# Turning the gated activations by DMA, as planes of 16-bit halves, instead of on TensorE

## The chip, the cores and the metric

The kernel runs on one core of one Trainium2 chip. The metric is the device time of one execution in microseconds (us). The engines are named as the profile names them: PE is TensorE (PEld its weight loads), DVE is VectorE, ACT is ScalarE, POOL is GpSimd, SP is SyncE. PE, DVE and ACT do the arithmetic here; SP and POOL, and now ACT too, issue DMAs.

## The reference

One layer of a decoder: RMSNorm, three token mixers, merged by gates and projected, with a residual; then RMSNorm and a SwiGLU feed-forward layer with a residual. The change touches the feed-forward part only:

```python
D_MODEL = 2048; SEQ = 256; D_FF = 5632
h2 = rmsnorm(x, g_ffn)                       # 256 x 2048, float32
gu = h2 @ w_gu                               # 256 x 11264
x = x + (jax.nn.silu(gu[..., :D_FF]) * gu[..., D_FF:]) @ w_down
```

The gated activations `a = silu(g) * u` are 256 x 5632 in float32. The product with `w_gu` leaves the 256 tokens on partitions; the product with `w_down` needs `a` with the feed-forward index on partitions. So every block of `a` has to be transposed.

## The kernel before

The kernel is written in Python over a tile framework. The framework allocates the tiles, puts in the semaphores, and orders each engine's instructions by a planner that works with estimated durations; `keep_in_program_order` pins an instruction to its place. Each engine then runs its own instructions strictly in order.

Each float32 product is done as three reduced-precision matmuls (`product`, lines 164 to 169): high part times high part (L167), high times low (L168), low times high (L169). So every block of weights is split before use (`split`, L104 and L105): ACT casts it into `w_hi`, DVE subtracts to get `w_lo`. A block of weights is 128 x 2 x 512 float32, and there are five buffers each of `w_hi` and `w_lo`. ACT can split a block only when PE has read the buffer of five blocks before.

The stage that matters computes `g` and `u`. It is a loop over 11 chunks `c` of 512 feed-forward columns. `project_pair` computes one chunk for both halves of the tokens, with one level of a Strassen-like scheme on part of the blocks; it makes 22 weight blocks by calls of `parts`, eighteen for its own chunk and four (`begin_pair`) ahead for the next. In the order of the program the blocks are: f5 (two, from the tile `u`), two plain ones (`w_raw`), f6 (two, `u`), a plain one, f7 (two, `g_raw`), a plain one, f3 (two, `g_raw`), two plain ones, f4 (two, `u`), two plain ones, and the four of `begin_pair` (`g_raw`). A form block is read by six matmuls, a plain one by twelve: 180 matmuls in a chunk.

Small side jobs are generators in the list `stages`. Each call of `parts` runs the one at the front of the list to its next `yield` (`advance`). That is how `to_a(c, sg)`, appended after chunk `c`, is spread over the blocks of chunk `c+1`. `sg` are two tiles of 128 tokens x 512 columns, written by ACT (silu, L959) and DVE (L960).

Before the change `to_a` transposes with PE: `transpose4` (L185) does four 128 x 128 transposes of one `sg` tile into a PSUM tile `tr` (L189). For the chunks that are used first in the next stage (`ORDER[:EARLY]`, chunks 0, 1 and 2) `a.put` splits the result straight out of PSUM into `a_hi` and `a_lo`. For the other eight, ACT copies it into an SBUF tile (L950) and POOL issues its store to `a_mem` in device memory (L951), to be fetched and split in the next stage. `half_kb()` gives 128 x 512 float32 tiles out of twelve buffers.

During this stage SP issues the weight loads (L102), and POOL issues the stores of `a_mem` and two accumulating DMAs per chunk (L360).

Of the kernel before, what the change touches and what calls it, by code (L numbers as in the profile page):

```python
# [8 lines left out]

F32 = mybir.dt.float32  # L10
F32R = mybir.dt.float32r
AF = mybir.ActivationFunctionType
ALU = mybir.AluOpType
AX = mybir.AxisListType
# [3 lines left out]
P = 128  # L18
D = 2048
S = 256  # L20
NT = S // P
# [5 lines left out]
D_FF = 5632  # L27
NF = D_FF // P
NB = 512
# [25 lines left out]
def hybrid_block(ctx: ExitStack, tc: tile.TileContext, x, g_mix, w_in, q_gain, k_gain, w_branch, w_out,  # L55
                 g_ffn, w_gu, w_down, rel_bias, onehot, extra, out):
    nc = tc.nc
# [20 lines left out]
    def pool(stack, name, side, bufs=1):  # L78
        return stack.enter_context(tc.tile_pool(name=name, bufs=bufs, side=side, reuse_waits="tile"))

    h2_stack, ph1, pm, pgx = ExitStack(), ExitStack(), ExitStack(), ExitStack()
# [6 lines left out]
    def half_kb(dt=F32):  # L88

        return scratch.tile([P, NB], dt, name="sc")  # L90
# [13 lines left out]
    def split(hi, lo, src, pin=False):  # L104
        for op in nc.scalar.copy(hi, src), nc.vector.tensor_sub(lo, src, hi.bitcast(F32)):  # L105
            if pin:
                tc.keep_in_program_order(op)
# [5 lines left out]
    def raw_weights(w, row0, c, col0):  # L113
        raw = wpool.tile([P, 2, NB], F32, name="w_raw", bufs=4)
        return raw, nc.sync.dma_start(raw, block(w, row0 // P + c, col0))

    def weights(w, row0, k0, nk, col0, there=()):

        for i, c in enumerate(range(k0, nk, 2)):
            raw = there[i] if i < len(there) else raw_weights(w, row0, c, col0)[0]  # L120
            hi = wpool.tile([P, 2, NB], F32R, name="w_hi")
            lo = wpool.tile([P, 2, NB], F32R, name="w_lo")
            split(hi, lo, raw)
# [47 lines left out]
    def rsqrt_mean(dst, ss, n, cols):  # L171
# [3 lines left out]
        y = small.tile([P, cols], F32, name=f"rs_y{cols}")  # L175
        nc.scalar.activation(y, v, AF.Ln)
        nc.scalar.activation(y, y, AF.Exp, scale=-0.5)
        t = small.tile([P, cols], F32, name=f"rs_t{cols}")
# [6 lines left out]
    def transpose4(src):  # L185

        pt = tr.tile([P, 4, P], F32, name="tr")
        for i in range(4):
            nc.tensor.transpose(pt[:, i, :], src[:, i * P:(i + 1) * P], ident)  # L189
        return pt  # L190


    class Columns:


        def __init__(self, pl, name, nk):
            self.hi, self.lo = (pl.tile([P, nk, S], F32R, name=f"{name}_{n}") for n in ("hi", "lo"))

# [20 lines left out]
    class Sums:  # L219
# [8 lines left out]
        def place(self, pl, c):  # L228
            self.s[c] = [pl.tile([P, 4, S], F32R, name=f"{self.name}_s{n}{c}") for n in ("hi", "lo")]

# [14 lines left out]
    class Chunks(Sums):  # L245
# [9 lines left out]
        def place(self, pl, c):  # L255
            if c in self.wc:
                super().place(pl, c)
                self.t[c] = [[pl.tile(sh, F32R, name=f"{self.name}_{t}{n}{c}") for n in ("hi", "lo")]
                             for t, sh in enumerate(([P, 4, P], [P, 2, P]))]
            else:  # L260
                self.t[c] = [pl.tile([P, 4, S], F32R, name=f"{self.name}_{n}{c}") for n in ("hi", "lo")]

# [137 lines left out]
    h = Columns(p1, "h", KT)  # L400
# [13 lines left out]
    def to_h(acts, src, c, t, g, by_scalar=False):  # L414
# [3 lines left out]
        if by_scalar:  # L418
            for i in range(4):
                nc.scalar.activation(tmp[:, i], pt[:, i], AF.Copy, scale=g[:, 4 * c + i:4 * c + i + 1])  # L420
        else:
# [4 lines left out]
    def squares(xc, dst, c, pin=False):  # L426
        for t in range(NT):
            sq = nc.scalar.activation(half_kb(), xc[t], AF.Square, accum_out=dst[:, t, c:c + 1])
            if pin:
# [85 lines left out]
    with tc.manual_schedule(engines={mybir.EngineType.PE, mybir.EngineType.DVE, mybir.EngineType.Activation}):  # L515
# [16 lines left out]
        turned = [transpose4(xs[1][0])]  # L532
# [103 lines left out]
    def stick_breaking(hl, qT, kT, v):  # L636
# [7 lines left out]
        l = pa.tile([P, n], F32, name="p", bufs=1)  # L644
        nc.scalar.activation(l, z[:, :n], AF.Abs)
        nc.scalar.activation(l, l, AF.Exp, scale=-1.0)
        nc.scalar.activation(l, l, AF.Ln, bias=1.0)
# [267 lines left out]
    pm.close()  # L915
    pr = pool(ctx, "pr", "right")
    gd = pool(ctx, "gd", "right", 4)
    rstd2 = small.tile([P, NT], F32, name="rstd2", bufs=1)

    def second_norm():  # L920
# [11 lines left out]
    a_mem = dram.tile([NF // 4, P, 4, S], F32, name="a_mem")  # L932

    WD = (4, 6, 8)
    ORDER = [0, 1, 2, 4, 3, 6, 5, 8, 7, 9, 10]
    EARLY = 3
    a = Chunks(None, "a", NF // 4, WD, False)

    for c in ORDER[:EARLY]:
        a.place(pe, c)  # L940

    def to_a(c, srcs):
        for t in range(NT):
            pt = transpose4(srcs[t])
            if c in ORDER[:EARLY]:
                a.put(c, t, pt)
                yield
                continue
            st = half_kb().rearrange("p (k q) -> p k q", k=4)
            nc.scalar.copy(st, pt)  # L950
            nc.gpsimd.dma_start(a_mem[c, :, :, t * P:(t + 1) * P], st)  # L951
            yield

    for c in range(D_FF // NB):
        nxt = (h2, w_gu, (c + 1) * NB, D_FF + (c + 1) * NB) if c + 1 < D_FF // NB else None
        (g0, g1_, u0, u1), ahead = project_pair(h2, w_gu, c * NB, D_FF + c * NB, ahead, nxt)
        sg = [half_kb() for _ in range(NT)]
        for t, (g, u) in enumerate(((g0, u0), (g1_, u1))):
            nc.scalar.activation(sg[t], g, AF.Silu, scale=rstd2[:, t:t + 1])  # L959
            nc.vector.scalar_tensor_tensor(sg[t], u, rstd2[:, t:t + 1], sg[t], op0=ALU.mult, op1=ALU.mult)  # L960
        stages.append(to_a(c, sg))
# [179 lines left out]
```

## Time and profile before

| what | value |
|---|---|
| median of three runs | 1362.64 us (1362.42 to 1362.77) |
| the profiled execution | 1362.37 us |
| its span, first to last instruction | 1360.7 us |
| busy: PE, DVE, ACT | 1352.9, 1150.0, 878.8 us |
| granted TensorE clock | 1.0 throughout |
| mean DMA traffic | 241 GB/s |

Shares of busy time are means over the whole span. A line of the profile names engine, line of the kernel, operation, output and inputs, and the idle time of the engine ahead of it with what ended it. Busy times of PE include the pipelined ends of matmuls, so a sum of durations is more than the time that they take one behind another; the distance between two starts is what a matmul costs.

### The profile page before, as it was taken

The page shows a single profiled execution, that of the slowest core. Times are in us where ns is not written, and L with a number is a line of the kernel's source. Part 1 is how long each engine was busy: PE and PEld are TensorE (multiplying, and loading weights), DVE is VectorE, ACT ScalarE, POOL GpSimd, SP SyncE. Part 2 cuts the span into 40 slices and gives each one's busy share as a digit, 9 for nine tenths or more (in the row PEclk, how much of TensorE's full clock was granted, in tenths as well). Part 3 has the DMA queues.
Part 4 walks back from the last instruction along what each step waited for, and adds up shares of the span by engine and source line. Part 5 has one row for each costly group of instructions (what it writes and reads, how often), then busy time and mean ns, then how long its engine had stood idle before and what let it go on. Part 6 is the DMA issues. An engine that isn't in the chain of part 4 may idle for free.

```text
span 1360.7 us, 17886 instructions
## 1 busy us (share of the span) xinstructions
PE 1352.9 (99%) x6404; PEld 1181.1 (87%) x6404; DVE 1150.0 (85%) x1225; ACT 878.8 (65%) x1137; POOL 103.0 (8%) x164
## 2 busy tenths in 40 slices
PE   9999999999999999999999999999999999999998
PEld 7888888888888888888888888888888888888887
DVE  7888797866998887876789999999999998896885
ACT  7677877766876765445557666766666675664453
POOL 1100000000011112100100000010000010000000
PEclk9999999999999999999999999999999999999999
DMA  8775657566778788877797777778787876787653
GB/s 281 286 250 163 229 156 262 143 216 229 247 256 287 247 257 300 298 238 222 233 331 260 257 237 250 224 250 278 253 271 254 272 214 221 240 290 258 200 178 102
DMA packets 93016, 327.92 MB, mean 241 GB/s; under 512 B 11168, under 2 KB 12784, under 8 KB 92928
## 3 DMA queue, kind: packets, MB, share of 16 engines
q1 hardware_dynamic: 76896, 275.29, 58.0%
q0 software_dynamic: 14848, 50.45, 14.6%
q8 instruction: 50, 0.82, 0.2%
q10 hardware_dynamic: 1184, 1.06, 0.2%
q14 instruction: 38, 0.31, 0.1%
HBM read 291.08 MB, written 14.70 MB: 225 GB/s over the span
## 4 chain that ended last, share of the span: by engine, by line
PE 94%; ACT 3%; DVE 2%; issue 1%; DMA 0%; DVEq 0%; ACTq 0%
PE ps L167 11%; PE ps L169 11%; PE ps L168 11%; PE qs L169 11%; PE qs L168 11%; PE qs L167 11%; PE z L168 4%; PE z L169 4%; PE z L167 4%; PE v L167 3%; PE v L168 3%; PE v L169 3%; PE tr L189 2%; PE tr L168 1%; PE tr L169 1%; PE tr L167 1%
## 5 line engine op out<-in xcount | busy, mean ns | idle before, releaser
L105 DVE TENSOR_TENSOR w_lo<-w_raw,w_hi 128x1024 fp32r<-128x1024 f32 x334 | 405.3, 1222 | 82.0 <-ACT w_hi L105 79.5
L105 ACT CAST w_hi<-w_raw 128x1024 fp32r<-128x1024 f32 x334 | 347.6, 1048 | 176.5 <-PE qs L169 79.6
L105 ACT CAST w_hi<-g_raw 128x1024 fp32r<-128x1024 f32 x184 | 191.6, 1049 | 145.2 <-PE ps L169 44.9
L105 DVE TENSOR_TENSOR w_lo<-g_raw,w_hi 128x1024 fp32r<-128x1024 f32 x184 | 220.8, 1223 | 37.8 <-ACT w_hi L105 35.3
L105 ACT CAST w_hi<-u 128x1024 fp32r<-128x1024 f32 x138 | 143.9, 1048 | 81.1 <-DVE u L1041 15.6
L105 DVE TENSOR_TENSOR w_lo<-u,w_hi 128x1024 fp32r<-128x1024 f32 x138 | 167.3, 1222 | 26.4 <-ACT w_hi L105 25.8
L168 PE MATMUL ps<-w_lo,h_hi 128*128 128x512 f32 x360 | 136.7, 380 | 0.0
L169 PE MATMUL ps<-w_hi,h_lo 128*128 128x512 f32 x360 | 136.5, 379 | 0.0
L167 PE MATMUL ps<-w_hi,h_hi 128*128 128x512 f32 x360 | 134.1, 383 | 0.0
L168 PE MATMUL qs<-w_lo,h_hi 128*128 128x512 f32 x332 | 126.4, 381 | 0.0
L169 PE MATMUL qs<-w_hi,h_lo 128*128 128x512 f32 x332 | 125.9, 380 | 0.0
L167 PE MATMUL qs<-w_hi,h_hi 128*128 128x512 f32 x332 | 122.5, 381 | 0.0
L169 PEld LDWEIGHTS ps<-w_hi,h_lo 128*128 128x128 f32 x360 | 68.0, 189 | 9.8 <-DVE h_lo L105 0.3
L168 PEld LDWEIGHTS ps<-w_lo,h_hi 128*128 128x128 f32 x360 | 68.1, 189 | 9.3
L167 PEld LDWEIGHTS ps<-w_hi,h_hi 128*128 128x128 f32 x360 | 67.8, 189 | 9.2
L169 PEld LDWEIGHTS qs<-w_hi,h_lo 128*128 128x128 f32 x332 | 62.8, 189 | 9.4 <-issue 0.6
L168 PEld LDWEIGHTS qs<-w_lo,h_hi 128*128 128x128 f32 x332 | 62.8, 189 | 9.0 <-DVE w_lo L105 0.4
L321 DVE TENSOR_TENSOR u<-g_raw 128x1024 f32<-128x1024 f32 x40 | 48.8, 1220 | 25.7 <-DMA g_raw<-in_w_in 18.4
L167 PEld LDWEIGHTS qs<-w_hi,h_hi 128*128 128x128 f32 x332 | 62.7, 189 | 8.6
L360 POOL DMA_DIRECT2D u<-g_raw x40 | 35.1, 878 | 232.1 <-DVE w_lo L105 165.8
L310 DVE TENSOR_TENSOR u<-u,g_raw 128x1024 f32<-128x1024 f32 x40 | 47.2, 1220 | 0.0
L310 DVE TENSOR_TENSOR g_raw<-g_raw 128x1024 f32<-128x1024 f32 x40 | 47.2, 1219 | 0.0
(400 smaller groups left out, 2940.1 us busy)
## 6 DMA issues: line engine op xcount, KB each, us to landing
w_raw<-in_w_in SPq DMA_DIRECT2D x118, 512.0 KB, 4.7
g_raw<-in_w_gu SPq DMA_DIRECT2D x88, 512.0 KB, 6.3
w_raw<-in_w_gu SPq DMA_DIRECT2D x88, 512.0 KB, 6.7
g_raw<-in_w_in SPq DMA_DIRECT2D x72, 512.0 KB, 6.1
w_raw<-in_w_down SPq DMA_DIRECT2D x64, 512.0 KB, 4.2
u<-g_raw POOLq DMA_DIRECT2D x40, 512.0 KB, 5.6
w_raw<-in_w_branch SPq DMA_DIRECT2D x32, 512.0 KB, 4.6
w_raw<-in_w_out SPq DMA_DIRECT2D x32, 512.0 KB, 4.2
```

Source lines behind the costliest of these rows:

```text
L105: for op in nc.scalar.copy(hi, src), nc.vector.tensor_sub(lo, src, hi.bitcast(F32)):
L167: nc.tensor.matmul(ps, ah, wh, start=start, stop=False, **how)
L168: nc.tensor.matmul(ps, ah, wl, start=False, stop=False, **how)
L169: nc.tensor.matmul(ps, al, wh, start=False, stop=stop, **how)
L189: nc.tensor.transpose(pt[:, i, :], src[:, i * P:(i + 1) * P], ident)
L310: tc.keep_in_program_order(nc.vector.tensor_add(d, d, a))
L321: nc.vector.tensor_add(d, a, b)
L360: nc.gpsimd.dma_start(d, a, accum_op=ALU.add)
```

## The change

Ten of the eleven chunks are no longer transposed on PE. For each `sg` tile of such a chunk, ACT copies the 512 float32 values of a row into 1024 values of 16 bits, the low halves of the words in one plane and the high halves in another (`halves`). A transposing DMA, issued by ACT, turns this 128 x 1024 tile of 16-bit values into eight 128 x 128 blocks (`turned`). ACT then joins the planes again into a float32 tile, by a pinned copy that writes 16-bit values with a step of two. From there the tile goes the old way: it is split for chunks 0 to 2 (now out of SBUF), and stored to `a_mem` by POOL for the others.

The work is spread over the calls of `parts`: the first tile's copy at call 1, its DMA at 2, the second tile's copy at 4, its DMA at 5, then a pause, the first join at 13 and the second at 15. `halves` and `turned` have two buffers each in a new pool `planes`. Chunk 10, the last, is transposed on PE as before.

```diff
+U16 = mybir.dt.uint16
...
+    planes = pool(h2_stack, "planes", "left", 2)
...
+    def keep_a(c, t, part):
+        if c in ORDER[:EARLY]:
+            a.put(c, t, part)
+        else:
+            nc.gpsimd.dma_start(a_mem[c, :, :, t * P:(t + 1) * P], part)
+
     def to_a(c, srcs):
+        if c == D_FF // NB - 1:
+            for t in range(NT):
+                pt = transpose4(srcs[t])
+                st = half_kb().rearrange("p (k q) -> p k q", k=4)
+                nc.scalar.copy(st, pt)
+                keep_a(c, t, st)
+                yield
+            return
+        turned = []
         for t in range(NT):
-            pt = transpose4(srcs[t])
-            if c in ORDER[:EARLY]:
-                a.put(c, t, pt)
-                yield
-                continue
-            st = half_kb().rearrange("p (k q) -> p k q", k=4)
-            nc.scalar.copy(st, pt)
-            nc.gpsimd.dma_start(a_mem[c, :, :, t * P:(t + 1) * P], st)
+            halves = planes.tile([P, 2, NB], U16, name="halves")
+            nc.scalar.copy(halves, srcs[t].bitcast(U16).rearrange("p (n h) -> p h n", h=2))
+            yield
+            turned.append(planes.tile([P, 8, P], U16, name="turned"))
+            nc.scalar.dma_start_transpose(turned[t], halves.rearrange("p h n -> p (h n)"))
+            yield
+            yield
+        for _ in range(6):
+            yield
+        for t in range(NT):
+            st = half_kb()
+            tc.keep_in_program_order(nc.scalar.copy(
+                st.bitcast(U16).rearrange("p (k q h) -> p h k q", k=4, h=2),
+                turned[t].rearrange("p (h k) q -> p h k q", h=2)))
+            keep_a(c, t, st.rearrange("p (k q) -> p k q", k=4))
+            yield
             yield
```

## The prediction

> **What bounds the kernel now.** I read the page first, then the stage of the eleven chunks by windows of one chunk each.
>
> ```profile
> PE 1352.9 (99%) x6404; PEld 1181.1 (87%) x6404; DVE 1150.0 (85%) x1225; ACT 878.8 (65%) x1137; POOL 103.0 (8%) x164
> PE 94%; ACT 3%; DVE 2%; issue 1%; DMA 0%; DVEq 0%; ACTq 0%
> core 0: us, PE busy (x) PEld busy (x) DVE busy (x) ACT busy (x) POOL busy (x), PEclk, DMA share, GB/s
> 899.00:938.73 39.73, 39.73 (x190) 34.83 (x189) 36.51 (x35) 26.69 (x31) 4.43 (x6) 1.00 0.80 267
> 938.73:978.46 39.73, 39.73 (x190) 34.83 (x189) 36.68 (x35) 26.68 (x31) 3.25 (x4) 1.00 0.81 269
> 978.46:1018.19 39.73, 39.73 (x190) 34.83 (x189) 36.67 (x35) 26.68 (x31) 3.32 (x4) 1.00 0.74 251
> 1018.19:1057.92 39.73, 39.73 (x190) 34.83 (x189) 36.67 (x35) 26.68 (x31) 3.29 (x4) 1.00 0.76 248
> ```
>
> PE is busy 99% of the span and makes 94% of the chain that ended last. In the windows, one chunk takes 39.73 us and PE never stops; DVE is busy 36.7 us of them, ACT 26.7. So a PE slot that disappears is time won, as long as DVE (3.0 us spare per chunk) and ACT (13.0 us spare) still deliver on time. DVE is the engine to watch: it stands right behind PE.
>
> **What is removed from PE.** The order of time on PE around the transposes of one chunk:
>
> ```profile
> 903.71 0.60 PE L189 MATMUL tr<-ident,sc 128*128 128x128 f32 x4
> 904.06 0.46 PE L167 MATMUL z<-w_hi,h_shi 128*128 128x512 f32 x1
> 904.36 0.60 PE L189 MATMUL tr<-ident,sc 128*128 128x128 f32 x4
> 904.72 0.46 PE L167 MATMUL v<-w_hi,h_hi 128*128 128x512 f32 x1
> 905.02 0.38 PE L168 MATMUL z<-w_lo,h_shi 128*128 128x512 f32 x1
> 905.23 0.38 PE L169 MATMUL z<-w_hi,h_slo 128*128 128x512 f32 x1
> L189 PE MATMUL tr<-ident,sc x88: 272/272/273, 744.8 to 1144.8; 128*128 128x128 f32 x88
> ```
>
> The durations (0.27 us for a transpose, 0.38 for a matmul) overlap, so I go by starts. Two matmuls behind each other start 0.216 us apart (905.02 and 905.23 round it down). From 903.71 to 905.02 are 1.31 us with eight transposes and two matmuls; less 2 x 0.216 that leaves 0.88 us for eight transposes. The window agrees: 180 matmuls x 0.216 = 38.86 us, and 39.73 - 38.86 = 0.87. The last row counts 88 transposes in the stage, eight for each of eleven chunks; ten chunks lose theirs: 10 x 0.88 = 8.8 us off PE.
>
> **What is added on ACT, and what goes.** Durations of the nearest instructions:
>
> ```profile
> L105 ACT CAST w_hi<-w_raw 128x1024 fp32r<-128x1024 f32 x85 | 88.2, 1049 | 26.6 <-PE qs L169 14.3 <-PE ps L169 9.1 <-PE z L169 3.1
> L950 ACT COPY sc<-tr 128x512 f32<-128x512 f32 x14 | 8.3, 590 | 10.0 <-PE tr L189 9.5
> L1099 ACTq DMA_DIRECT2D out<-sc x8: 338/338/363, 1241.7 to 1357.3; - x8
> L951 POOL DMA_DIRECT2D a_mem<-sc x16: 724/762/871, 865.5 to 1146.4; - x16
> L102 SPq DMA_DIRECT2D w_raw<-in_w_in x76: 327/328/1784, 1.3 to 508.3; - x76
> ```
>
> A copy into halves, and a join, each write 1024 values per partition, as the cast of 1.05 us does; I take 1.05. Ends: 0.59, the copy of 512 values, and 2.10 if a 16-bit value with a step cost double. Two copies and two joins are 4.2 us per chunk, and two PSUM copies (1.18 us) go.
>
> The issue of a transposing DMA stands in no row. A plain one holds ACT for 0.34 us. POOL's issue, also for 256 KB, takes 0.76 us. The longest issue on SP is 1.78 us. [...] ACT per chunk: 26.7 - 1.2 + 4.2 + 2 x 0.76 = 31.2 us of 38.9, 80%. In sum it fits; the question is where the pieces stand, because DVE's `w_lo` and then PE wait behind every `w_hi` that is late.
>
> ```profile
> 940.72 2.00 ACT L105 CAST w_hi<-w_raw 128x1024 fp32r<-128x1024 f32 x2
> 944.07 1.25 ACT L950 COPY sc<-tr 128x512 f32<-128x512 f32 x2 [1.36 <-PE tr L189]
> 945.42 1.06 ACT L105 CAST w_hi<-u 128x1024 fp32r<-128x1024 f32 x1
> 946.86 1.05 ACT L105 CAST w_hi<-u 128x1024 fp32r<-128x1024 f32 x1
> 951.54 2.18 ACT L105 CAST w_hi<-g_raw 128x1024 fp32r<-128x1024 f32 x2 [2.69 <-DVE g_raw L310]
> 947.94 1.23 DVE L105 TENSOR_TENSOR w_lo<-u,w_hi 128x1024 fp32r<-128x1024 f32 x1 [0.20 <-ACT w_hi L105]
> 952.62 2.36 DVE L105 TENSOR_TENSOR w_lo<-g_raw,w_hi 128x1024 fp32r<-128x1024 f32 x2
> 956.62 0.38 PE L168 MATMUL qs<-w_lo,h_shi 128*128 128x512 f32 x1
> ```
>
> The tight place is the first third of a chunk, calls 1 to 6. Between 942.72 and the f6 cast at 945.42 ACT has 2.70 us in which it waits for the transposes or copies them; both vanish. Into this come two copies (2.10) and two issues of x us each, the second perhaps between the two f6 casts. The second f6 cast is then late by 2.10 + 2x - 2.70 = 2x - 0.6. DVE idles that much, since it stands in order at that `w_lo`. How much may it be? The first f7 `w_lo` ends at 952.62 + 1.22 = 953.84 and PE reads it at 956.62: a lead of 2.8 us, of which 0.88 is lost because PE no longer transposes before it. So 1.9 us of lateness is covered: x up to 1.25. With x = 0.76 it is late by 0.9 us, hidden. DVE over the chunk: 36.7 + 0.9 = 37.6 of 38.9 us; it catches up. Beyond x = 1.25, PE waits 2(x - 1.25) per chunk. With copies of 2.10 and x = 0.76 the lateness is 3.0, PE waits 1.1, and the change costs 0.2 x 10 = 2 us: that end and x = 1.78 (2 x 0.53 - 0.88 = 0.18 per chunk) both give about 1364.5.
>
> The joins stand at calls 13 and 15, where a plain block and f4 are split:
>
> ```profile
> 957.90 1.05 ACT L105 CAST w_hi<-w_raw 128x1024 fp32r<-128x1024 f32 x1 [0.62 <-PE qs L169]
> 961.35 1.05 ACT L105 CAST w_hi<-u 128x1024 fp32r<-128x1024 f32 x1 [0.62 <-PE z L169]
> 966.53 1.05 ACT L105 CAST w_hi<-w_raw 128x1024 fp32r<-128x1024 f32 x1 [1.54 <-PE qs L169]
> ```
>
> These three gaps alone are 2.78 us against 2.10 us of joins: hidden by gaps in which ACT waited for PE to free buffers. Without that cover they would cost at most 2.1 per chunk.
>
> A join also waits for its DMA, and behind it on ACT stand the casts of f4, for which DVE and PE wait. From call 2 to 13, and 5 to 15, are 11 and 10 of 22 calls, 19 and 18 us.
>
> ```profile
> a_mem<-sc POOLq DMA_DIRECT2D x16, 256.0 KB, 5.0
> sc<-x POOLq DMA_DIRECT2D x8, 256.0 KB, 8.2
> q1 hardware_dynamic: 76896, 275.29, 58.0%
> q10 hardware_dynamic: 1184, 1.06, 0.2%
> ```
>
> DMAs of this size land within 5.0 to 8.2 us (medians), less than half of that. The DMA engines' time: q1 moves 275.29 MB in 58% of the span, 2.9 us per MB, so 256 KB are at least 0.75 us. Pieces smaller than q10's: 0.2% of 16 x 1360.7 us for 1184 packets is 37 ns each. Cut into 1024 rows of 128 values that is 1024 x 37 ns / 16 = 2.4 us; cut further, into 8192 pieces as the turned blocks' short runs might be, 19 us. I take 2.4, the cut that the shapes name. The four windows' mean DMA share of 0.78 is 30.9 us; with 4.8 us it is 35.7 of 38.9, 92%. It still fits, so nothing is charged.
>
> Edits together: POOL's store goes to calls 13 and 15; the accumulating DMAs stand before it in the chunk, so nothing urgent queues behind. SP's queue is untouched. Chunks 0 to 2 get a join and a split out of SBUF in place of one out of PSUM, the same two instructions besides. The last chunk has 18 calls, and the work of the ninth needs 16.
>
> **Sum.** 1362.37 of the profiled execution (span 1360.7) - 8.8 + 0 = 1353.6. The median of the runs stands 0.27 above that execution: 1353.9.
>
> **Rivals.**
> 1. ACT is held longer by the issue. In this kernel that is x between 1.55 and 1.9: PE waits 0.6 to 1.3 us per chunk behind the late f6 and f7 splits and the 0.88 is eaten: at 1.7, 2 x 0.45 - 0.88 = 0.02, no change, 1362.8. For it: two issues per chunk sit in the tightest place. Against: no row of 256 KB is above 0.87. Chance 0.14. Between 1.25 and 1.55 (chance 0.12) the gain is partial, 1354 to 1360.
>    [...]
> 2. Slower: the DMA engines become the bound. Each chunk needs 30.9 us of their time; with y us per transposing DMA the chunk takes 30.9 + 2y once that is above 38.9, so from y = 4.0, and it is slower than before by over 0.2% from y = 4.6. At y = 6: 42.9 us, 3.2 us more per chunk, 1394. For it: the 8192 pieces; against: the 1024 rows. Chance 0.12. An issue above 1.9 us or doubled copies end on this side as well, at 1365 to 1380: 0.08.
> 3. The transposes leave and PE is no faster because DVE is the bound: it would have to lose over 3.0 us per chunk, against 0.9 expected. Held within case 1.
>
> **How the numbers follow.** My forecast has 0.54; with the partial gain faster is 0.66, no change 0.14, slower 0.20. About 0.2% (2.7 us) is what a measurement of this kernel can tell from no change. The range goes from 1352.5 (a transpose slot slightly dearer than read) to 1364.5, the bound of the issue and of the copies, which takes in case 1; it leaves out case 2 and the longer issues. The likeliest case's own range is 1352.5 to 1356.
>
> **What would show it.** Right: windows of one chunk of 38.9 us with PE at 100%, 8 transposes left in the stage, DVE near 36.5 busy. The issue shows as rows of ACT's queue: under 1.25 us. Wrong: idle of PE put down to DVE `w_lo` around the f6 and f7 forms (case 1), waits of ACT's joins or of ACT and DVE for weight DMAs with a DMA share near 1 (case 2).

## The result and the profile after

| | median, us | range of the runs, us |
|---|---|---|
| before | 1362.70 | 1362.42 to 1362.93 |
| after | 1356.09 | 1354.26 to 1357.02 |

The change makes the kernel faster: 0.995 of the time before (95% interval 0.9938 to 0.9962), 6.6 us less where 8.8 were forecast. The four runs lie 2.8 us apart, those of before 0.5. The profiled execution took 1355.54 us with a span of 1353.5, 7.2 less than before. All line numbers behind the new `U16` are one higher, and those behind `to_a` 25 higher.

From the page of after: busy times, the chain that ended last, and the DMA queues.

```profile
PE 1344.1 (99%) x6324; PEld 1171.8 (87%) x6324; DVE 1146.0 (85%) x1225; ACT 906.8 (67%) x1163; POOL 102.4 (8%) x164
PE 88%; ACT 3%; DMA 3%; issue 3%; DVE 2%; SPq 0%; ACTq 0%; DVEq 0%; POOL 0%; POOLq 0%
q1 hardware_dynamic: 76896, 275.29, 59.4%
q0 software_dynamic: 14848, 50.45, 15.4%
q10 hardware_dynamic: 22304, 6.30, 2.6%
```

PE issues 80 instructions fewer (6404 to 6324), the ten chunks' transposes. PE's share of the chain falls from 94% to 88%; DMA and issue, 0% and 1% before, now have 3% each. Something that PE waits for, if only a little, is new.

One chunk each by windows of after; the first is disturbed, the second is not.

```profile
core 0: us, PE busy (x) PEld busy (x) DVE busy (x) ACT busy (x) POOL busy (x), PEclk, DMA share, GB/s
780.10:818.88 38.78, 38.24 (x176) 32.55 (x175) 37.27 (x37) 30.15 (x35) 1.71 (x2) 1.00 0.84 257
896.25:935.10 38.85, 38.85 (x182) 34.02 (x181) 36.21 (x34) 29.27 (x33) 4.39 (x6) 1.00 0.92 272
```

In an undisturbed chunk PE never stops and takes 38.85 us (the window counts 182 matmuls, because two at its edges belong to the neighbours): the chunk of 39.73 us has lost its transposes at the forecast price. The DMA share, 0.74 to 0.81 in the four windows of before, is 0.91 to 1.02 in the six windows from 857 to 1091 us and 0.84 to 0.86 in the three ahead of them. A share of 1.02 (935.10 to 974.54 us) shows that the packets' times overlap, so a share is not purely time in which an engine could do nothing else.

All that PE waited for in the stage (total, times, longest), then what DVE waited for from DMAs, both from the waits of after.

```profile
PE v L169 <- DVE w_lo L106: 0.3, 1, 0.3
PE z L168 <- ACT sc L306: 0.2, 1, 0.2
DVE u L322 <- DMA g_raw<-in_w_gu: 5.3, 5, 2.0
```

DVE's waits for weight loads were 1.6 us in two before. PE's two waits stand 1.6 us apart in one chunk; by the distances of starts they cost 1.1 us, since the first two matmuls behind each wait start 0.32 us apart (786.98 and 787.30, 788.56 and 788.88) and not 0.216. Smaller delays, 0.1 us at 784 us and 0.2 us at 983 us, make it 1.3 us in the stage. This is the timeline there, ACT, DVE and PE:

```profile
784.61 1.06 ACT L106 CAST w_hi<-w_raw 128x1024 fp32r<-128x1024 f32 x1
784.75 1.25 ACTq L965 DMA_TRANSPOSE turned<-halves  x1
785.57 1.04 ACT L962 COPY halves<-sc 128x1024 uint16<-128x1024 uint16 x1
785.70 1.23 DVE L106 TENSOR_TENSOR w_lo<-w_raw,w_hi 128x1024 fp32r<-128x1024 f32 x1 [0.67 <-ACT w_hi L106]
786.64 1.25 ACTq L965 DMA_TRANSPOSE turned<-halves  x1
786.98 0.48 PE L169 MATMUL v<-w_lo,h_hi 128*128 128x512 f32 x1 [0.30 <-DVE w_lo L106]
787.92 0.59 ACT L306 COPY sc<-z 128x512 f32<-128x512 f32 x1 [1.32 <-issue]
787.94 0.38 PE L170 MATMUL v<-w_hi,h_lo 128*128 128x512 f32 x1
788.56 0.48 PE L168 MATMUL z<-w_hi,h_hi 128*128 128x512 f32 x1 [0.24 <-ACT sc L306]
```

ACT's copy of `z` out of PSUM (L306) has to be done before PE may write the next `z`, and for it PE waited at 788.56. ACT stood 1.32 us ahead of it, "issue" being time in which the profile shows nothing that it waited for: it was issuing the second transposing DMA from 786.64 to 787.89. The first issue (784.75 to 786.00) cost nothing: a cast was running until 785.67, and the copy behind it started at 785.57, during the issue.

The wait at 786.98 is another one. PE needs the `w_lo` of the second plain block there, whose cast (784.61) runs ahead of the second issue, so that issue has no part in it. In an undisturbed chunk this `w_lo` is done 1.1 us before PE reads it.

The same place in the timeline of an undisturbed chunk of after:

```profile
902.77 1.25 ACTq L965 DMA_TRANSPOSE turned<-halves  x1
904.06 0.59 ACT L306 COPY sc<-z 128x512 f32<-128x512 f32 x1 [1.32 <-issue]
905.24 0.38 PE L168 MATMUL z<-w_hi,h_hi 128*128 128x512 f32 x1
```

And in the timeline of the kernel before:

```profile
946.38 0.58 ACT L305 COPY sc<-z 128x512 f32<-128x512 f32 x1
948.42 0.38 PE L167 MATMUL z<-w_hi,h_hi 128*128 128x512 f32 x1
```

Before, the copy was done 948.42 - 946.96 = 1.46 us before PE came to its next `z`. Now it is 0.59 us. I call this the margin. It is used up where ACT is late for another reason: 0.05 us, PE waiting, at 788 and again at 983. Some 19 us ahead of the wait at 788, DVE had waited 1.79 us for a weight load, and ACT then waited 1.49 us for DVE at the start of the chunk (780.10):

```profile
769.09 1.23 DVE L322 TENSOR_TENSOR u<-g_raw 128x1024 f32<-128x1024 f32 x1 [1.79 <-DMA g_raw<-in_w_gu]
```

That load was not slow, it was issued late. By the trace it landed 5.2 us after its issue, while its kind has a median of 5.7. It stood in SP's queue behind a load that needed a `g_raw` buffer, and this buffer was free only when one of the chunk's two accumulating DMAs, which read `g_raw`, had landed at 763.42. That DMA had been issued at 751.75, with a transposing DMA still in flight until 756.64. SP's waits for accumulating DMAs in the stage, in after and in before:

```profile
SPq L103 <- DMA u<-g_raw: 21.5, 11, 3.3
SPq L102 <- DMA u<-g_raw: 6.3, 5, 3.8
```

The accumulating DMAs of the stage land 8.9 us after their issue (median), where before it was 6.5.

### The profile page after: what moved, and what is told of

The parts are those of the page before. It is cut to its first block, busy times and chain, and to the rows that moved or that the text cites. A ratio compares the mean times of both kernels' runs of the same rounds, so it can differ in the third digit from the quotient of the medians.

```text
span 1353.5 us, 17720 instructions
## 1 busy us (share of the span) xinstructions
PE 1344.1 (99%) x6324; PEld 1171.8 (87%) x6324; DVE 1146.0 (85%) x1225; ACT 906.8 (67%) x1163; POOL 102.4 (8%) x164
## 3 DMA queue, kind: packets, MB, share of 16 engines
q1 hardware_dynamic: 76896, 275.29, 59.4%
q0 software_dynamic: 14848, 50.45, 15.4%
q10 hardware_dynamic: 22304, 6.30, 2.6%
## 4 chain that ended last, share of the span: by engine, by line
PE 88%; ACT 3%; DMA 3%; issue 3%; DVE 2%; SPq 0%; ACTq 0%; DVEq 0%; POOL 0%; POOLq 0%
PE ps L170 10%; PE ps L168 10%; PE ps L169 10%; PE qs L170 10%; PE qs L168 10%; PE qs L169 10%; PE z L168 4%; PE z L170 4%; PE z L169 4%; PE v L168 2%; PE v L169 2%; PE v L170 2%; PE tr L170 1%; DVE w_lo L106 1%; PE tr L169 1%
```

## The experiments

What is to be explained is the 2 us that are missing, and the spread. The theories: A, the issue holds ACT; B, the transposes' traffic delays other loads; C, the copies and joins are too much for ACT. D came out of the first experiments: A and B only together.

**The changed kernel again, beside its parts.** Same kernel as after.

> The changed kernel itself, again. Its four times so far spread over 2.8 us (1354.26 to 1357.02), those of the kernel before over 0.5 us, and the forecast of 1353.9 was missed by 2.2 us at the median. Theory A (ACT is held by the two issues of 1.25 us per chunk) has no reason for a spread: 1356 with one PE wait of some 1.2 us at the same place in every profile. Theory B (the transposing DMAs bring the DMA engines near to full, weight loads land late in some executions) expects times spread over 2 to 3 us again, and PE waits at other places than at 786 us. Both: 1354 to 1357.

1355.66 us (1354.25 to 1357.90), ratio 0.9948 (0.9936 to 0.9961). Its profiled execution lost time in three chunks, at 786, 903 and 983 us, by 0.5 to 0.8 us each, PE's start-up included, each time at this wait (waits of this run, whole time from the stage on):

```profile
PE z L168 <- ACT sc L306: 0.7, 3, 0.2
```

In two of the three, 0.2 to 0.3 us of the loss stands one step earlier, at the `w_lo` of the second plain block. Ahead of each, ACT or DVE had waited 1.2 to 2.2 us for a load or for an accumulating DMA. One more chunk is hit than in the first profile, and the sum differs (2.0 us against 1.3), which fits a spread that comes from late transfers.

**Nothing turned.**

```diff
-            (halves, copy, transposing DMA, pauses, join)
+            # chunks 0 to 2: a.put(c, t, srcs[t]); others:
+            nc.scalar.copy(st, srcs[t])
```

> The ceiling: the ten chunks' PE transposes are left out and nothing stands in their place (ACT copies or splits the gated activations straight from SBUF, so they go on unturned). Both theories: all of the 8.8 us off PE and nothing that is late: 1362.7 - 8.8 = 1353.9, spread like before (0.5 us). Were it 1356, the 8.8 us themselves would be mis-sized.

1354.52 us (1353.55 to 1355.63), ratio 0.9939 (0.9926 to 0.9951), PE without a wait from the stage on. The spread is 2.1 us, not the 0.5 expected, although nothing is turned: so not all of the changed kernel's spread comes from the change. No run here shows where the rest comes from.

**Copies and joins, without the DMA.**

```diff
-            turned.append(planes.tile([P, 8, P], U16, name="turned"))
-            nc.scalar.dma_start_transpose(turned[t], halves.rearrange("p h n -> p (h n)"))
+            turned.append(halves.rearrange("p h (k q) -> p (h k) q", k=4))
```

> The changed kernel without its transposing DMAs: the joins read the halves directly, so the activations go on unturned; the four copies of ACT per chunk stay. Theories A and B: 1353.9, small spread, since both the issue and the traffic are gone. Theory C (the copies, 1.05 and 1.35 us against the two of 0.59 removed, are what delays DVE and PE): 1356, as the changed kernel.

1353.87 us (1353.52 to 1354.77), ratio 0.9935 (0.9923 to 0.9948). The windows of this run:

```profile
895.85:934.70 38.85, 38.85 (x182) 34.02 (x181) 36.25 (x35) 29.51 (x33) 4.40 (x6) 1.00 0.81 246
```

ACT is as busy as after (29.51 against 29.27 us), PE has no wait, the margin is 1.58 us in every chunk, and 8.7 us are gained (1362.56 in the runs of before beside it). The copies and joins cost nothing where loads are on time: C falls. What is missing hangs on the DMA.

**Both ways at once.** PE's transposes are put back beside the additions.

```diff
             nc.scalar.copy(halves, srcs[t].bitcast(U16).rearrange("p (n h) -> p h n", h=2))
+            pt = transpose4(srcs[t])
+            # a.put for chunks 0 to 2, copy and store for the others, as before
```

> Everything that the change adds (copies, transposing DMAs, joins) stands beside the PE transposes, and its result is not used; so nothing is won, and the price of the additions shows alone. By the prediction's working with 1.25 + 0.07 us for an issue: 2.10 + 2 x 1.32 of work against 1.36 us of idle time of ACT in the first third of a chunk (the copies out of PSUM stay) is 3.4 us late against a lead of 2.8: theory A has PE wait 0.6 us per chunk, 1362.7 + 6 = 1369. Theory B: what the changed kernel missed, 2.2 us, and no more: 1365, spread over 2 to 3 us. If the additions are wholly hidden: 1362.7.

1365.31 us (1364.97 to 1369.94), ratio 1.0031 (1.0022 to 1.004): all that the change adds costs 2.75 us where it doesn't replace anything. Taken with 8.7, that leaves about 6, near the 6.6 gained. Six of its eleven runs lie within 0.4 us and five are 1.7 to 4.6 us above these, so here too the cost differs from run to run. The median is theory B's number; its spread is wider than B said.

**The transposing DMAs from SP's queue.**

```diff
-            nc.scalar.dma_start_transpose(turned[t], ...
+            nc.sync.dma_start_transpose(turned[t], ...
```

> The transposing DMAs issued by SP instead of ACT, all else as changed. ACT is no longer held; the traffic stays. Theory A (PE waits because ACT's copy of z out of PSUM stands behind the two issues): those waits go, 1353.9. Theory B (weight loads late because of the traffic): 1355.7 as the changed kernel, and SP's own queue, in which the transposes now wait for ACT's copies, can add to it.

1426.93 us (1426.05 to 1429.35), ratio 1.0477 (1.0462 to 1.0491), 64 us slower than before. SP's timeline in this run:

```profile
903.57 2.88 SPq L103 DMA_DIRECT2D g_raw<-in_w_gu  x6
926.57 1.24 SPq L965 DMA_TRANSPOSE turned<-halves  x1
927.90 1.00 SPq L103 DMA_DIRECT2D w_raw<-in_w_gu  x2
```

SP stood at the transpose for 20 us, until its `halves` was written, with the next chunk's weight loads queued behind. The issue here is as long as on ACT (1.24 us); over all twenty it is 1.24 to 2.66 us, median 1.48. So this does not take the hold alone away, as it was meant to: it puts a wait into the one queue that feeds everything. The mean granted clock was 0.979 to 0.982 in its four runs and 0.999 or 1.0 in those of before; whether a part of the 64 us is the clock's is not shown.

**The second DMA three calls later, pinned.**

```diff
+            if t:
+                for _ in range(3):
+                    yield
...
+            keep = tc.keep_in_program_order if t else (lambda op: op)
+            keep(nc.scalar.copy(halves, ...
+            keep(nc.scalar.dma_start_transpose(turned[t], ...
-        for _ in range(6):
+        for _ in range(3):
```

> The second tile's copy and its DMA are pinned behind the split of the block ahead of f7, so that its issue stands behind the copy of z and the f6 casts, in a stretch where ACT waited 2.86 us for DVE. Theory A: no PE wait at the first z matmul after f5, 1353.9, spread under 1.5 us. Theory B: the traffic is the same, 1355.7 and the same spread.

1361.13 us (1360.5 to 1362.1), ratio 0.9992 (0.9983 to 1.0): nearly all of the gain gone, which no theory had said. The group of the transposing DMAs (its columns: least, median and longest issue in ns, first and last start):

```profile
L969 ACTq DMA_TRANSPOSE turned<-halves x20: 1247/1344/2447, 744.2 to 1109.3; - x20
```

The timeline of ACT and DVE there:

```profile
912.55 2.45 ACTq L969 DMA_TRANSPOSE turned<-halves  x1
915.04 0.58 ACT L306 COPY sc<-ps 128x512 f32<-128x512 f32 x1 [1.51 <-issue]
916.61 1.23 DVE L106 TENSOR_TENSOR w_lo<-g_raw,w_hi 128x1024 fp32r<-128x1024 f32 x1 [1.82 <-ACT w_hi L106]
```

In its new place the DMA has a semaphore instruction of its own ahead of it (ten on ACT's queue, one per chunk), and its issue takes up to 2.45 us between the f7 casts; why it is longer there is not shown. Behind it stand a copy out of PSUM and the second f7 cast, for which DVE waits. The margin at the copy of `z` is back at 1.54 to 1.59 in all ten chunks, as theory A wanted, but by starts PE loses some 6.7 us at other places of the stage; the largest single delay, 1.1 us, is behind such a copy out of PSUM. What a hold costs depends on what stands behind it; this run moved it from a bad place to a worse one.

**The traffic alone.** Four plain DMAs of 256 KB from POOL's queue in place of each transposing one.

```diff
+            turned.append(halves.rearrange("p h (k q) -> p (h k) q", k=4))
+            for _ in range(4):
+                nc.gpsimd.dma_start(planes.tile([P, 2, NB], U16, name="copied"), halves)
```

> The changed kernel with each transposing DMA replaced by four plain DMAs of the same 256 KB, issued by POOL, whose result is not used (the joins read the halves, the activations go on unturned): 8 x 256 KB more per chunk, which at 0.75 us each raises the DMA share by about 0.15, as the transposes did, and ACT is not held. Theory A: 1353.9, as without any DMA. Theory B: 1355 to 1357.

1358.20 us (1356.95 to 1362.51), ratio 0.9973 (0.9964 to 0.9983): 4.3 us above the run without DMAs, with no issue on ACT. Its waits:

```profile
ACT w_hi L106 <- DMA g_raw<-in_w_gu: 10.4, 9, 2.1
PE v L169 <- DVE w_lo L106: 0.9, 3, 0.3
```

Traffic of this size makes weight loads late by up to 2.3 us (2.1 at ACT, 2.3 at DVE), and by starts PE loses 3.9 us in the stage, with the largest delays three times at the `w_lo` of the second plain block. This is the place of the wait at 786.98 of after, and this run has no issue on ACT: added transfers alone can cost time. It is no clean copy of the change's traffic, because POOL issues the accumulating DMAs too: it is busy 7.6 us in a window of one chunk (895.85 to 934.70), 4.4 in that of after.

**The hold alone.** Four tiny DMAs from ACT's queue in place of each transposing one.

```diff
+            for i in range(4):
+                nc.scalar.dma_start(planes.tile([P, 16], U16, name=f"bit{i}"), halves[:, 0, 16 * i:16 * i + 16])
```

> The changed kernel with each transposing DMA replaced by four DMAs of 4 KB issued by ACT (0.34 us each, 1.36 us together) whose result is not used; the joins read the halves, the activations go on unturned. ACT is held as long as by the transposes, with hardly any traffic; the planner puts the second four behind the copy of z, between the two f6 casts. Theory A: held behind the z copy rather than before it, f6 late by 2.1 us against a lead of about 1.9: 1354 to 1356. Theory B: 1353.9.

1362.81 us (1361.84 to 1364.67), ratio 1.0004 (0.9995 to 1.0013). The four issues (0.61 us each at the median, not 0.34) held ACT 2.5 us, twice what I wanted, and the planner put the second four between the two f6 casts (timeline of ACT):

```profile
906.77 2.50 ACTq L966 DMA_DIRECT2D bit<-halves  x4
909.30 1.04 ACT L106 CAST w_hi<-u 128x1024 fp32r<-128x1024 f32 x1 [1.55 <-DMA bit<-halves]
```

What PE waited for in this run:

```profile
PE qs L169 <- DVE w_lo L106: 2.8, 5, 0.8
PE ps L169 <- DVE w_lo L106: 2.7, 5, 0.7
```

It doesn't weigh A against B, but it shows the prediction's path at work: the f6 cast late, then `w_lo`, then PE, in all ten chunks (2.8 and 2.7 us in five each, 0.67 to 0.94 by starts). At 2.5 us of hold it eats the whole 8.8.

**The second DMA behind the first f6 cast.** The same transfers, the second of them issued later.

```diff
-            nc.scalar.dma_start_transpose(turned[t], ...
+            turn = nc.scalar.dma_start_transpose(turned[t], ...
+            if t:
+                tc.keep_in_program_order(turn)
```

> The changed kernel with the second transposing DMA pinned behind the first f6 cast; the order of ACT is otherwise the same, and no other DMA is waited for. The sequencer then issues while the cast runs, as it does for the first tile, and the copy of z is not held. Theory D (joint: the second issue, 1.32 us in which ACT stands still ahead of the copy of z, leaves PE a margin of 0.55 us there, and weight loads that land 1.3 to 2.2 us late use it up in two or three chunks of ten): the margin is near 1.9 us again, PE waits only where loads are later than that, 1353.9 to 1354.5, spread under 1.5 us. Theory B (late loads alone): 1355.7 and a spread of 2 to 3 us, as the changed kernel.

Median 1354.42 us, ratio 0.9949 (0.9936 to 0.9963). Ten of eleven runs lie from 1353.62 to 1356.02, a spread of 2.4 us where under 1.5 was expected, and one at 1365.18. The timeline of ACT and PE:

```profile
901.34 0.59 ACT L306 COPY sc<-z 128x512 f32<-128x512 f32 x1 [0.33 <-PE z L170]
902.50 1.05 ACT L106 CAST w_hi<-u 128x1024 fp32r<-128x1024 f32 x1 [0.57 <-DVE u L311]
902.51 1.25 ACTq L965 DMA_TRANSPOSE turned<-halves  x1
903.80 1.05 ACT L106 CAST w_hi<-u 128x1024 fp32r<-128x1024 f32 x1 [0.25 <-DVE u L311]
903.52 0.38 PE L168 MATMUL z<-w_hi,h_hi 128*128 128x512 f32 x1
```

DVE's waits for loads in this run:

```profile
DVE u L322 <- DMA g_raw<-in_w_gu: 3.5, 5, 1.3
```

The copy of `z` is done at 901.93, 1.59 us before PE's next `z`, as without the DMA. The issue runs while the cast handed over just before it runs, and ACT then waits for DVE almost as long in any case: the second f6 cast starts 1.30 us behind the first, against 1.14 in the run without the DMA. Loads are still late (3.5 us, up to 1.3), and PE has no wait. So late loads of up to 1.3 us cost nothing when the margin is whole.

This doesn't clear the larger ones, because the edit moved more than the hold. The second transposing DMA now starts 1.0 us ahead of PE's `z`, not 2.5, and the transposes land sooner (median 5.0 us, after had 7.3). So do the accumulating DMAs (7.1 against 8.9 in the stage), and SP hardly waits for them:

```profile
SPq L103 <- DMA u<-g_raw: 3.1, 4, 1.2
```

Ahead of each chunk that lost 0.2 us or more in the two profiles of the changed kernel, the waits for loads and accumulating DMAs add up to 2.0 us or more; here they are 1.3 at most. So this run does not show what sums as large would cost without the hold.

**The hold without late loads.** The two accumulating DMAs of each chunk are left out in this stage; the issue stays in its place.

```diff
-        for d, a in zip(u, b21):
-            nc.gpsimd.dma_start(d, a, accum_op=ALU.add)
+        if w is not w_gu:
+            for d, a in zip(u, b21):
+                nc.gpsimd.dma_start(d, a, accum_op=ALU.add)
```

> The changed kernel without the two accumulating DMAs of each chunk of this stage (1 MB out of one buffer and into another; u then lacks one term). The hold of ACT ahead of the copy of z stays, the traffic falls by some 4 to 6 us of the DMA engines' time per chunk, back to that of the kernel before. Theory A (the hold alone): 1355.7. Theories B and D: no late loads, so no PE wait: 1353.9, spread under 1.5 us.

1353.63 us (1353.54 to 1354.82), ratio 0.9938 (0.9926 to 0.9951). Waits of ACT and of DVE:

```profile
ACT sc L306 <- issue: 13.2, 10, 1.4
DVE u L322 <- DMA g_raw<-in_w_gu: 0.2, 1, 0.2
```

The hold is there in all ten chunks, 1.32 us each, the margin is 0.54 to 0.60 in each, the loads are on time, and PE has no wait in the stage. The hold alone costs nothing: A alone falls. The edit takes away just the DMAs for which SP waited in after, so the late loads hang on them, by their place in this chain or by their traffic.

**Changed kernel and moved hold, side by side on one chip.** The unchanged kernel, and the edit of the second DMA behind the f6 cast again.

> The changed kernel once more, on the same chip as the next kernel, because the two were timed on different occasions so far and their intervals overlap. Theory D: 1355.5 to 1356, spread 2 to 3 us, margin at the copy of z near 0.55 us, PE waits where loads were late. If chips or occasions made the difference: the same as the next kernel.

> The second transposing DMA pinned behind the first f6 cast, once more, on the same chip as the changed kernel. Theory D: 1354.2 to 1354.5, 1.2 to 1.7 us below it, spread under 1.5 us, margin 1.58 us. If occasions made the difference: within 0.5 us of it.

The changed kernel: 1357.45 us (1354.04 to 1359.65), ratio 0.9965 (0.9953 to 0.9977). The moved hold: 1353.88 us (1353.66 to 1361.86), ratio 0.9949 (0.9933 to 0.9966). Five of its six runs lie within 1.2 us, from 1353.66 to 1354.82; the changed kernel's are spread over 5.6. The profile of the changed kernel fell on its fastest run (1354.04): no load was late by more than 0.33 us, the margins were 0.40 to 0.60, PE had no wait. In the profile of the moved hold loads were late by up to 1.44 us, the margin stayed 1.58, and PE had no wait either. So what made the changed kernel's four slower runs (1356.8 to 1359.65) slow is not seen in this profile. The medians are 3.6 us apart, more than the 1.2 to 1.7 expected; the intervals of the ratios overlap because of single high runs (1361.86 here, 1365.18 in the first try). Over all occasions the changed kernel has a median of 1356.2 in fifteen runs, and the moved version 1354.2 in seventeen; eight of the fifteen lie above 1356.02, but only two of the seventeen. These two are the high ones, and their mean granted clock, 0.997, is the lowest of both versions. Were the time to go with the clock, 0.3% of the span would be some 4 us, an estimate, and only a part of the 8 and 11 us by which they are higher; the rest stays open.

## Why the prediction was right, and where its sizes were off

The forecast was 1353.9 with its own range to 1356; the median is 1356.09, just past that end, and well inside the whole range. Faster, the likeliest sign, is what came. By its number the result also lies in the partial gain of 1354 to 1360, to which 0.12 was given for an issue between 1.25 and 1.55 us; but the path of that case, the late f6 split, did not cost the time.

- **What leaves PE: right.** 10 x 0.88 = 8.8 us. (The working's 180 x 0.216 is 38.88, not 38.86, which changes nothing.) Chunks without a disturbance take 38.85 us, 8.7 us are gained when the DMA alone is left out, and the changed kernel's fastest runs (1354.04, 1354.08) have nearly all of it.
- **Copies: right.** 1.05 us taken, 1.045 measured. **Joins: under-sized, without effect.** 1.05 taken, 1.35 measured, and the planner ran both behind the 17th of the 22 blocks, not at calls 13 and 15. The run without the DMA shows them to be hidden.
- **The issue: mis-sized.** x was taken as 0.76, between 0.33 and 1.78. That a transposing DMA's issue on ACT would cost what POOL's issue of a plain 256 KB does (L951 of before, median 762 ns) was the author's estimate. The groups of tile `turned` and line L972 of after:

```profile
L965 ACTq DMA_TRANSPOSE turned<-halves x20: 1246/1247/1363, 744.3 to 1097.2; - x20
L972 ACT COPY sc<-turned x20: 1332/1348/1362, 765.8 to 1118.0; 128x1024 uint16<-128x1024 uint16 x20
DMA to landing us min/median/max: 5.1/7.3/11.4
```

1.247 us, which is the very threshold of 1.25 that the working gave. Of the two issues per chunk only one is exposed, for 1.32 us: the first overlaps a cast and a copy, while the second waits for the copy just ahead of it (in the chunk shown the copy ends at 786.61 and the issue starts at 786.64), and ACT runs nothing until 787.92. Two issues of 0.76 (1.52) and one of 1.32 are close, so the sum survived. That was luck: the working counted both as exposed, and with 1.25 us each they would have used the whole cover.
- **The tight place: wrong.** The working followed the hold from the f6 cast over `w_lo` to PE and found 1.9 us of cover. The planner put the second issue one step earlier, ahead of ACT's copy of `z` out of PSUM, which PE needs sooner: its margin was 1.46 us before, and it was not priced. The hold takes it to 0.59, where it is 1.58 without the DMA. That alone costs nothing, but 0.6 us is all that remains for any other lateness. The f6 path is real (the four tiny DMAs show it), and wasn't reached.
- **DMA engines, "it still fits, so nothing is charged": the step that failed.** The cut into about 1024 rows was right: q10 has (22304 - 1184) / 20 = 1056 packets more per DMA. The 8192 pieces of the dearer cut were a supposition, and no run shows them. Its share rose by 2.4% of 16 engines' 1353.5 us, 1.6 us per DMA and engine. The other queues' packets became slower too: q1 moves the same bytes in 59.4% instead of 58.0%, and q0, of which before had this row,

```profile
q0 software_dynamic: 14848, 50.45, 14.6%
```

takes 15.4%. Over the whole span q0 and q1 together need 1012 us per engine instead of 988, 1.2 us more per transposing DMA, so 2.85 in all where 2.4 was taken (in the other two profiles of the same kernel 2.2 and 2.7). The windows' share, 0.91 to 0.97 in most chunks from 857 to 1091 us, is near the forecast 0.92. But a mean share below 1 does not make the transfer free. Over the whole span the median landing time of the accumulating DMAs rises from 5.6 to 7.8 us and that of the plain weights from 6.7 to 7.9, while that of the `g_raw` loads falls from 6.3 to 5.7. Yet it is `g_raw` loads that come 1.1 to 2.2 us late, in two or three chunks of ten: SP issues them behind a load that must wait until an accumulating DMA has freed its buffer (21.5 us of such waiting against 6.3). "Nothing urgent queues behind" and "SP's queue is untouched" missed this link. A mean was used where the latest transfer decides.
- **Rival 1** (ACT held by the issue) had the right resource, and its threshold was not passed (1.247 us against 1.55): its 1362.8 did not come. **Rival 2** (DMA engines) named the right resource, but not the way in which it costs: no steady bound, only late transfers in some chunks. **Rival 3** did not arise: DVE has 36.2 us of 38.85.

So 8.7 to 8.8 us were won, and about 2 us at the median (from next to nothing to 5.7, by the run) given back. The two profiles that show a loss put it in chunks where a late accumulating DMA, or a load that waited for one, made ACT late. By starts some two thirds of their 3.3 us stand at the copy of `z`, whose margin the second issue has shortened; with 1.58 us each of these waits, at most 0.4 us, would have been covered. The rest stands at the `w_lo` ahead of it, where the issue has no part. So in these two profiles D holds for the larger part of the loss, and theory B alone for the smaller. Leaving the accumulating DMAs out (1353.6) or moving the second issue (1353.9 and 1354.4) ends the loss. How much of the second gain is the margin's and how much comes from transfers that land sooner is not separated, and neither is whether the transfers are late by the packets' number or by their time on the engines.

## What to carry to other kernels

When an instruction that issues a DMA goes onto an engine that computes, look for what stands directly behind it and how early that is needed: here a DMA issued for 1.25 us ahead of a copy out of PSUM went with 2 us lost, and the same DMA behind a cast, one step later, with next to none. Such a move also shifts the transfer in time, so look at both. Two small things, each hidden by itself, can use up the same margin; so subtract each of them from it before calling either free. A mean DMA share doesn't say whether each transfer is in time (it was 0.86 in the window in which DVE waited 1.79 us for a load): price the latest landing, and follow it to the buffer that it frees and the next load that waits for this buffer.

## What the runs showed of the hardware that was not expected

- An issue on ACT's queue cost ACT's arithmetic next to nothing while work ahead of it still ran: 0.16 us behind the f6 cast (1.30 us between the starts of the two f6 casts, 1.14 in the run without the DMA). Where it had to wait for the instruction just ahead, as in after, ACT stood for the full 1.25 us (1.32 with the gap), ten times in the stage.
- The issue of a transposing DMA of a 128 x 1024 tile of 16-bit values took 1.247 us on ACT (median of after), 3.7 times the 0.34 us of a plain one of 128 KB there. It was longer elsewhere: up to 2.45 us on ACT in the run with the DMA three calls later, and 1.24 to 2.66 us on SP.
- ACT's copies of 1024 16-bit values took 1.04 us where the step is in the input and 1.35 us where it is in the output (medians of twenty each in after, 1.045 and 1.348).
- The 256 KB of one transpose cost each DMA engine 1.6 us in its own packets, against 0.75 us for a plain 256 KB (an estimate: 58.0% of 1360.7 us for q1's 275.29 MB in before). The packets of the other queues took longer too, by 0.6 to 1.2 us per transpose in the three profiles of the changed kernel.
- The transposes landed 5.0 and 5.1 us after their issue (median) where the two of a chunk were issued 3.4 us apart (the two runs of the moved hold), and 6.3 to 7.3 us where they were 1.9 us apart (the three of the changed kernel).
